# Loading the modulation weights from GpSimd's queue, and token-major projections with 512 instead of 256 columns per product

## The chip, the cores and the metric

The kernel runs on one core of a Trainium2 chip. A core has TensorE (matrix products, results in PSUM), VectorE, ScalarE and GpSimd, and SyncE (SP), which here only issues DMA transfers. SP, ScalarE and GpSimd each have a queue in program order; an instruction waits there for its semaphores and holds up what stands behind it. The metric is the device time of one execution in microseconds (us).

## The reference

The model has two layers on 256 latent and 256 context tokens of 1024 features. Every layer is a SwiGLU half-step, a token mixer and another SwiGLU half-step; shift, scale and gate of each come from modulation vectors. The mixer is neighbourhood attention beside a Hyena convolution in layer 0, and retention in layer 1.

```python
def modulate(x, gain, shift, scale):
    return rms_norm(x, gain) * (1 + scale) + shift

def swiglu(h, w_in, w_out):
    a, b = jnp.split(h @ w_in, 2, axis=-1)
    return (jax.nn.silu(a) * b) @ w_out
...
    for i in range(DEPTH):
        mod_l = (jax.nn.silu(c) @ w_mod[i] + b_mod[i]).reshape(b, N_MOD, 1, D_MODEL)
        mod_c = (jax.nn.silu(c_ctx) @ w_mod[i] + b_mod[i]).reshape(N_MOD, 1, D_MODEL)
        x_lat = x_lat + 0.5 * mod_l[:, 2] * swiglu(modulate(x_lat, norm_gain[i, 0], mod_l[:, 0], mod_l[:, 1]),
                                                 ffn_a_in[i], ffn_a_out[i])
...
def retention_mixer(h_lat, h_ctx, w_in, w_out, logit_f, logit_b, rope_cos, rope_sin, ctx_out):
    def project(hh):
        q, k, v, g = jnp.split(hh @ w_in, [RET_QK, 2 * RET_QK, 2 * RET_QK + RET_V], axis=-1)
...
    def output(y, g, dtype):
...
        return (jax.nn.silu(g) * y) @ w_out
```

Only the latent stream of the last layer is returned.

## The kernel before

**Layout.** Activations lie feature-major: a tile has 128 features on the partitions and 512 columns, 256 latent and 256 context tokens. The normalised input of a layer's part is `H`, 8 such blocks, each as a pair of fp32r tiles, `hhi` (rounded) and `hlo` (the rest). Weights are split likewise into `whi` and `wlo`. Every product of two split operands is three products of TensorE: hi by hi, hi by lo, lo by hi (`mm3`, lines 208 to 210; the third of them is the first that reads `wlo`).

**Weights.** All weight tiles come in one order (`worder`). `w_dma` loads a tile of 512 or 704 KB into one of 4 `raw` buffers by SP's queue (line 138). `w_split` has ScalarE write `whi` and VectorE `wlo` (lines 152 and 153; 4 buffers each). `w_get` hands a tile to TensorE and has the splits issued up to three tiles ahead.

**FFN.** `ffn` goes through two halves of 11 pairs of weight tiles. `in_tile` makes one 128 x 512 product of a tile with `H`, in PSUM as `pi` (24 products of TensorE). `evac` has ScalarE and VectorE make `sg`, then split it into `ghi` and `glo`, so that 11 gate tiles collect. `out_gemm` multiplies them with 8 out-tiles, in the order of the gate tiles: the last gate tile is read by the products 31 to 33 of each out-tile.

**Modulation.** Layer 0's first shift and scale are made by TensorE at the start (`mods`). The other 128 tiles of modulation weights, 128 x 1024 each, are reduced by VectorE: `mod_step` multiplies a tile `wm` with the conditioning vector `scb`, one instruction per stream (line 237, output `junk`). The calls lie between the pairs of the FFN (two steps each) and behind the first four out-tiles of `out_gemm`. `m_dma` loads a tile into one of two buffers; `mod_step` calls it right after the reductions, for the tile after this one, so a tile's load is written in the program one step ahead of its use. In the first FFN, steps begin once the Hyena filter's tables have been split (`parted`, line 637), which GpSimd's four subtractions `flo` do.

**Token-major projections.** Three projections are wanted with tokens on the partitions: the values of the attention (`mixer0`, around line 1149), and values and gates of each retention head (`tok_proj`, line 1316, called by `tiles`). There `H` is the stationary operand, 128 features by 128 tokens, and the weights move. A weight tile of 128 x 1024 holds four blocks of features by 256 columns, as `tok_tiles` in `_layout` lays it out on the host; two tiles cover the 1024 features of one half of the 512 columns. For a head, four weight tiles make the values of four token tiles (`pv`), four more the gates of two (`pg`), with the scores of the next head and the output of this one between.

**Order.** Each engine runs its instructions in the order in which this program writes them; nothing reorders them later.

Of the kernel before, what the change touches and what calls it, by code (L numbers as in the profile page):

```python
# [16 lines left out]
P = 128  # L17
D = 1024
KB = D // P
# [35 lines left out]
def body(ctx, tc, I, out):  # L55
    nc = tc.nc
    V, S, T, SY, G = nc.vector, nc.scalar, nc.tensor, nc.sync, nc.gpsimd
# [16 lines left out]
    def page(shape=None, dt=F32, name="page"):  # L74
        tag = free.pop(0)
        low[0] = min(low[0], len(free))
        t = pagep.tile(shape or [P, TOK], dt, tag=tag, name=name)
        held[id(t)] = (tag, t)
        return t
# [5 lines left out]
    def ps(shape=None, name="ps"):  # L85
        return psp.tile(shape or [P, 512], F32, tag="ps", name=name)
# [55 lines left out]
    def w_split():  # L142
        i = wpos["split"]
        if i >= len(worder):
            return
        while wpos["dma"] <= i:
            w_dma()
        n = worder[i][1]
        t = raws.pop(i)
        hi = whl.tile([P, WSLOT], F32R, tag="hi", name="whi")  # L150
        lo = whl.tile([P, WSLOT], F32R, tag="lo", name="wlo")
        act(hi[:, :n], t[:, :n], AF.Copy)
        V.tensor_tensor(out=lo[:, :n], in0=t[:, :n], in1=f(hi[:, :n]), op=ALU.subtract)  # L153
        hls[i] = (hi, lo)
        wpos["split"] += 1
        if not hold[0]:
            w_dma()
# [14 lines left out]
    def w_get(ahead=3):  # L172
        i = wpos["get"]
        while wpos["split"] <= min(i + ahead, len(worder) - 1):
            w_split()
        wpos["get"] += 1
        return hls.pop(i)
# [39 lines left out]
    def m_dma():  # L217
        n = mpos["dma"]
        if n >= len(mlist):
            return  # L220
        t = modp.tile([P, D], F32, tag="wm", name="wm")
        SY.dma_start(out=t, in_=I["wmt"][n])
        mtile[n] = t
        mpos["dma"] += 1

    def mod_step(n=1):
        for _ in range(n):
            i = mpos["get"]
            if i >= len(mlist):
                return  # L230
            while mpos["dma"] <= i:
                m_dma()
            l, idx, b = mlist[i]
            t = mtile.pop(i)
            bcol = cst[:, C_BMOD + l * 72 + idx * 8 + b:C_BMOD + l * 72 + idx * 8 + b + 1]
            for s in range(1 if (l == 1 and idx >= 5) else 2):
                V.tensor_tensor_reduce(out=junk, in0=t, in1=scb[:, s, :], scale=1.0, scalar=bcol,  # L237
                                       op0=ALU.mult, op1=ALU.add,
                                       accum_out=MOD[l][:, idx, b, s:s + 1])
            mpos["get"] += 1  # L240
            m_dma()
# [669 lines left out]
    def mixer0(norm_in, norm_out):  # L911
# [34 lines left out]
        def z_conv(j, p, first):  # L946
            c = conv(p, (4 if first else 8) + j, "x1c" if first else "vc")
            b = next(c)
            yield
            next(c, None)  # L950
            if first:
                z[j] = b
                return
            V.tensor_tensor(out=z[j], in0=z[j], in1=b, op=ALU.mult)
            drop(b)
# [170 lines left out]
        def qk_step(again=False):  # L1126
            if todo:
                w, pp = todo.pop(0)
                sq = sqs.pop(0)
                if todo:  # L1130
                    sqs.append(qk_sq(todo[0][1]))
                qk_norm(w, pp, sq, ps(name="qss") if again else pso.tile([P, 512], F32, tag="po", name="qss"))
# [7 lines left out]
        pv = [ps(name="pv") for _ in range(4)]  # L1140
        for c in range(2):
            w = [w_get(), w_get(2)]
            for tb in range(4):
                o = pv[tb][:, c * 256:(c + 1) * 256]
                hs_ = slice(tb * P, (tb + 1) * P)
                for k in range(KB):
                    wk = w[k // 4]
                    ws_ = slice(k % 4 * 256, (k % 4 + 1) * 256)
                    T.matmul(o, lhsT=H[k][0][:, hs_], rhs=wk[0][:, ws_], start=k == 0, stop=False)
                    T.matmul(o, lhsT=H[k][0][:, hs_], rhs=wk[1][:, ws_], start=False, stop=False)  # L1150
                    T.matmul(o, lhsT=H[k][1][:, hs_], rhs=wk[0][:, ws_], start=False, stop=k == KB - 1)
                if c == 0 and tb in (0, 2):
                    qk_step()
# [33 lines left out]
        for i in range(12):  # L1187
            p = in_tile()
            attend(i)
            if i < 8:  # L1190
                ex, nor = left.pop(0)
                c = z_conv(i // 2, p, i % 2 == 0)
# [26 lines left out]
        for i in range(2):  # L1219
            t = page(dt=F32R, name="dfthi"), page(dt=F32R, name="dftlo")  # L1220
# [13 lines left out]
        for s in range(2):  # L1234
            for cb in range(4):
                inv(cb, s, py[cb])
                if s:
                    t = x0c[cb].rearrange("p s t -> p (s t)")
# [8 lines left out]
        out_gemm([cat[i] for i in range(KB)], KB, 1, 0, 1, False, norm_out)  # L1247

    mixer0(nm[0, 1], nm[0, 2])
    ffn(0, 2, nm[0, 2], nm[1, 0])  # L1250
    ffn(1, 0, nm[1, 0], nm[1, 1])


    def mixer1(norm_in, norm_out):
# [32 lines left out]
        for h in range(4):  # L1287
            pa, pb = in_tile(0, L), in_tile(0, L)
            q = page(name="qT")
# [23 lines left out]
            return dl, dc  # L1313


        def tok_proj(ntb, po, w, kh):
            for tb in range(ntb):
                for k4 in range(4):
                    k = kh * 4 + k4
                    hs_ = slice(tb * P, (tb + 1) * P)  # L1320
                    ws_ = slice(k4 * 256, (k4 + 1) * 256)
                    T.matmul(po[tb], lhsT=H[k][0][:, hs_], rhs=w[0][:, ws_], start=k == 0, stop=False)  # L1322
                    T.matmul(po[tb], lhsT=H[k][0][:, hs_], rhs=w[1][:, ws_], start=False, stop=False)  # L1323
                    T.matmul(po[tb], lhsT=H[k][1][:, hs_], rhs=w[0][:, ws_], start=False, stop=k == KB - 1)  # L1324
# [28 lines left out]
            return pt  # L1353

        def tiles(ntb, po, n):
            c, kh = divmod(n, 2)
            tok_proj(ntb, [q[:, c * 256:(c + 1) * 256] for q in po], w_get(), kh)

        def pv_norm(h, qb, pt, vh):
            p = ps(name="po")  # L1360
# [43 lines left out]
        for h in range(4):  # L1404
            if h < 3:
                qk_parts(h + 1)
            pv = [ps(name="pv") for _ in range(4)]
            for n in range(4):
                tiles(4, pv, n)
                if n == 0 and prev:  # L1410
                    o_trans(h - 1, prev)
            vh = []
            for tb in range(4):
                vh.append((page(dt=F32R, name="vhi"), page(dt=F32R, name="vlo")))
                split_to(pv[tb], *vh[tb])
            pg = [ps(name="pg") for _ in range(2)]
            tiles(2, pg, 0)
            if h < 3:
                npt = scores(h + 1)
            tiles(2, pg, 1)  # L1420
            os = [pv_norm(h, qb, pt, vh) for qb in range(2)]
            tiles(2, pg, 2)
            tiles(2, pg, 3)
            for a in vh + pt:
                drop(*a)
            for qb in range(2):
                gate_mul(os[qb], pg[qb])
            S.preload_act_table_set(LOG_SET)
            prev = os
            pt = npt  # L1430
# [16 lines left out]
    for b in range(KB):  # L1447
        c = slice(b % 2 * L, (b % 2 + 1) * L)
# [4 lines left out]
def _layout(inp):  # L1453
# [27 lines left out]
    t = np.linspace(0.0, 1.0, L, dtype=f4)  # L1481
    w = (f4(2.0 * math.pi) * np.arange(L, dtype=f4) / f4(L)).astype(f4)
# [28 lines left out]

    def tok_tiles(w):
        C = w.shape[1]
        return w.reshape(2, 4, P, C // 256, 256).transpose(3, 0, 2, 1, 4).reshape(C // 256 * 2, P, D)

    we = g["even_in"][0]
    fe = feat_tiles(we, 0)
# [1 line left out]
    hyo = [16, 20, 17, 21, 18, 22, 19, 23, 12, 13, 14, 15]  # L1519
    eo = g["even_out"][0]  # L1520
    z["ev"] = np.concatenate([fe[order], tok_tiles(we[:, 1024:1536]), fe[hyo], feat_tiles(eo, 0)])
    wr = g["ret_in"][0]
    perm = np.concatenate([h * 256 + np.concatenate([np.arange(64), 128 + np.arange(64), 64 + np.arange(64),
                                                     192 + np.arange(64)]) for h in range(4)])
    wq, wk = wr[:, :1024][:, perm], wr[:, 1024:2048][:, perm]
    vt, gt = tok_tiles(wr[:, 2048:4096]), tok_tiles(wr[:, 4096:6144])
    wo = g["ret_out"][0]
    o2 = np.stack([feat_tiles(wo[:D], 0), feat_tiles(wo[D:], 0)], axis=1).reshape(16, P, D)
# [14 lines left out]
    r, c = np.divmod(np.arange(L), 64)  # L1543
# [34 lines left out]
```

## Time and profile before

| | before |
|---|---|
| median of 3 runs | 1894.0 us (1890.67 to 1895.0) |
| profiled execution | 1885.11 us |
| its span, first to last instruction | 1883.3 us |
| TensorE busy | 1862.5 us, 99% of the span |
| VectorE busy | 1206.5 us, 64% |
| ScalarE busy | 701.3 us, 37% |
| GpSimd busy | 65.6 us, 3% |
| transfers of `wm` tiles for VectorE | 128 of 512 KB, all from SP's queue |
| transfers issued by GpSimd | 8 of 256 KB |

Busy is the time in which at least one instruction of an engine runs, from the start to the modelled end of each. Products on TensorE overlap, so that the distance of their starts, not their duration, tells how many fit in a stretch. A wait is counted when an engine has nothing running; "idle" in brackets behind an instruction is such a wait, with what ended it.

### The profile page before, as it was taken

How to read it: one execution, taken by the hardware profiler on the slowest of the kernel's cores; microseconds unless marked ns; L12 is line 12 of the kernel's file. 1: busy time of each engine (PE TensorE's matmuls, PEld its weight loads, DVE VectorE, ACT ScalarE, POOL GpSimd, SP SyncE). 2: the span in 40 equal slices, each digit the busy share in tenths (PEclk: the TensorE clock that was granted, in tenths of full speed). 3: DMA queues.
4: the chain of work that ended last, by engine and by line, in shares of the span. 5: the costliest groups of instructions: out<-in, count | busy, mean ns of one | idle time of the engine just before them, and what ended most of it. 6: DMA issues, size and time to landing. Idle time of an engine off the chain costs nothing.

```text
span 1883.3 us, 26318 instructions
## 1 busy us (share of the span) xinstructions
PE 1862.5 (99%) x10646; PEld 1607.7 (85%) x10646; DVE 1206.5 (64%) x1858; ACT 701.3 (37%) x1085; POOL 65.6 (3%) x73
## 2 busy tenths in 40 slices
PE   8999999999999999999999999999999999999999
PEld 5788888798877898788878988888889999999999
DVE  5577677777687767776766655433356755567554
ACT  4332122245474342212223422122234454455342
POOL 1010000002003000000000000000000111000000
PEclk9999999999999999999999999999999999999999
DMA  9345455532323325554564356323323423355663
GB/s 362 129 168 190 163 173 178 201 108 79 101 68 101 134 80 185 191 183 157 179 208 138 112 194 220 101 89 109 105 83 103 133 90 101 103 182 186 192 185 130
DMA packets 77899, 277.52 MB, mean 147 GB/s; under 512 B 8657, under 2 KB 9681, under 8 KB 77650
## 3 DMA queue, kind: packets, MB, share of 16 engines
q1 hardware_dynamic: 76626, 273.76, 43.7%
q0 software_dynamic: 1152, 2.10, 0.4%
q8 instruction: 83, 1.36, 0.3%
q14 instruction: 38, 0.31, 0.0%
HBM read 274.77 MB, written 1.05 MB: 146 GB/s over the span
## 4 chain that ended last, share of the span: by engine, by line
PE 84%; DVE 6%; DMA 6%; issue 2%; ACT 1%; SPq 0%; POOL 0%; DVEq 0%; POOLq 0%; ACTq 0%
PE pi L208 12%; PE pi L209 12%; PE pi L210 12%; PE po L209 9%; PE po L210 9%; PE po L208 9%; DMA wm<-in_wmt_dram 6%; DVE wlo L153 3%; PE fg L208 2%; PE fg L210 2%; PE fg L209 2%; PE pv L1322 2%; PE pv L1323 2%; PE pv L1324 2%; DVE junk L237 1%
## 5 line engine op out<-in xcount | busy, mean ns | idle before, releaser
L208 PE MATMUL pi<-hhi,whi 128*128 128x512 f32 (+1 forms) x1488 | 544.2, 366 | 0.0
L209 PE MATMUL pi<-hlo,whi 128*128 128x512 f32 (+1 forms) x1488 | 543.9, 366 | 0.0
L210 PE MATMUL pi<-hhi,wlo 128*128 128x512 f32 (+1 forms) x1488 | 543.1, 365 | 0.0
L153 DVE TENSOR_TENSOR wlo<-raw,whi 128x1024 fp32r<-128x1024 f32 (+1 forms) x325 | 421.5, 1313 | 164.3 <-ACT whi L89 164.1
L89 ACT ACTIVATE whi<-raw 128x1024 fp32r<-128x1024 f32 (+1 forms) x329 | 364.3, 1116 | 399.2 <-PE po L209 160.5
L237 DVE CUSTOM_DVE_ANT_0 junk<-wm,scb,cst 128x1024 bf16<-128x1024 f32 x224 | 291.1, 1299 | 84.0 <-DMA wm<-in_wmt_dram 80.1
L208 PEld LDWEIGHTS pi<-hhi,whi 128*128 128x128 f32 x1488 | 279.3, 188 | 51.7 <-issue 1.5
L210 PEld LDWEIGHTS pi<-hhi,wlo 128*128 128x128 f32 x1488 | 279.3, 188 | 48.8
L209 PEld LDWEIGHTS pi<-hlo,whi 128*128 128x128 f32 x1488 | 279.4, 188 | 48.1
L208 PE MATMUL po<-ghi,whi 128*128 128x512 f32 (+1 forms) x770 | 269.3, 350 | 1.1 <-ACT ghi L89 1.1
L209 PE MATMUL po<-glo,whi 128*128 128x512 f32 (+1 forms) x770 | 268.4, 349 | 0.7 <-DVE glo L181 0.7
L210 PE MATMUL po<-ghi,wlo 128*128 128x512 f32 (+1 forms) x770 | 268.4, 349 | 0.0
L89 ACT ACTIVATE ghi<-sg 128x512 fp32r<-128x512 f32 (+1 forms) x88 | 50.9, 579 | 378.8 <-DVE sg L580 375.7
L208 PEld LDWEIGHTS po<-ghi,whi 128*128 128x128 f32 x770 | 144.8, 188 | 22.2 <-ACT ghi L89 2.0
L209 PEld LDWEIGHTS po<-glo,whi 128*128 128x128 f32 x770 | 144.9, 188 | 21.9 <-DVE glo L181 1.6
L210 PEld LDWEIGHTS po<-ghi,wlo 128*128 128x128 f32 x770 | 144.9, 188 | 20.2
L391 DVE SCALAR_TENSOR_TENSOR x<-po,gate,x 128x256 f32<-128x256 f32 x136 | 61.3, 480 | 120.5 <-PE po L210 120.2
L580 DVE TENSOR_TENSOR sg<-sg,pi 128x512 f32<-128x512 f32 (+1 forms) x79 | 49.1, 621 | 104.3 <-PE pi L210 102.7
L181 DVE TENSOR_TENSOR glo<-sg,ghi 128x512 fp32r<-128x512 f32 (+1 forms) x88 | 55.1, 626 | 56.9 <-ACT ghi L89 56.9
L89 ACT ACTIVATE sq<-x 128x256 f32<-128x256 f32 (+1 forms) x71 | 30.2, 439 | 115.7 <-DVE x L391 115.6
L1322 PE MATMUL pv<-whi,hhi 128*128 128x256 f32 x256 | 72.2, 282 | 0.0
L1323 PE MATMUL pv<-wlo,hhi 128*128 128x256 f32 x256 | 71.7, 280 | 0.0
(332 smaller groups left out, 2392.1 us busy)
## 6 DMA issues: line engine op xcount, KB each, us to landing
raw<-in_ffi_dram SPq DMA_DIRECT2D x176, 512.0 KB, 3.7
wm<-in_wmt_dram SPq DMA_DIRECT2D x128, 512.0 KB, 4.4
raw<-in_ffo_dram SPq DMA_DIRECT2D x64, 704.0 KB, 4.4
raw<-in_rt_dram SPq DMA_DIRECT2D x64, 512.0 KB, 3.7
raw<-in_ev_dram SPq DMA_DIRECT2D x32, 512.0 KB, 3.5
wm<-in_wm_dram SPq DMA_DIRECT2D x32, 256.0 KB, 5.6
x<-in_xt_dram SPq DMA_DIRECT2D x8, 256.0 KB, 5.0
bias<-in_rpb_dram SPq DMA_DIRECT2D x8, 256.0 KB, 4.0
```

Source lines behind the costliest of these rows:

```text
L89: S.activation(out=out, in_=in_, func=func, **k)
L153: V.tensor_tensor(out=lo[:, :n], in0=t[:, :n], in1=f(hi[:, :n]), op=ALU.subtract)
L181: V.tensor_tensor(out=lo, in0=src, in1=f(hi), op=ALU.subtract)
L208: T.matmul(o, lhsT=w[0][:, c0:c1], rhs=x[0][:, x0:x1], start=start, stop=False)
L209: T.matmul(o, lhsT=w[0][:, c0:c1], rhs=x[1][:, x0:x1], start=False, stop=False)
L210: T.matmul(o, lhsT=w[1][:, c0:c1], rhs=x[0][:, x0:x1], start=False, stop=stop)
L237: V.tensor_tensor_reduce(out=junk, in0=t, in1=scb[:, s, :], scale=1.0, scalar=bcol, op0=ALU.mult, op1=ALU.add, accum_out=MOD[l][:, idx, b, ...
L391: V.scalar_tensor_tensor(out=xs(s, m), in0=p[:, c0:c0 + L], scalar=gate[:, m, s:s + 1], in1=xs(s, m), op0=ALU.mult, op1=ALU.add)
L580: V.tensor_tensor(out=sg, in0=sg, in1=pb[:, :w], op=ALU.mult)
L1322: T.matmul(po[tb], lhsT=H[k][0][:, hs_], rhs=w[0][:, ws_], start=k == 0, stop=False)
L1323: T.matmul(po[tb], lhsT=H[k][0][:, hs_], rhs=w[1][:, ws_], start=False, stop=False)
L1324: T.matmul(po[tb], lhsT=H[k][1][:, hs_], rhs=w[0][:, ws_], start=False, stop=k == KB - 1)
```

## The change

The loads of modulation tiles are issued by GpSimd's queue (`G`) instead of SP's (`SY`). And in the three token-major projections a product takes 512 columns of weights instead of 256: a weight tile now holds two blocks of features by 512 columns, and four tiles cover the 1024 features of all 512 columns. The number of weight tiles and their size stay; the accumulators are the same.

```diff
@@ def m_dma
         t = modp.tile([P, D], F32, tag="wm", name="wm")
-        SY.dma_start(out=t, in_=I["wmt"][n])
+        G.dma_start(out=t, in_=I["wmt"][n])
@@ mixer0
             for tb in range(4):
-                o = pv[tb][:, c * 256:(c + 1) * 256]
+                o = pv[tb]
                 hs_ = slice(tb * P, (tb + 1) * P)
-                for k in range(KB):
-                    wk = w[k // 4]
-                    ws_ = slice(k % 4 * 256, (k % 4 + 1) * 256)
+                for k in range(4 * c, 4 * c + 4):
+                    wk = w[k // 2 % 2]
+                    ws_ = slice(k % 2 * 512, (k % 2 + 1) * 512)
@@ mixer1
-        def tok_proj(ntb, po, w, kh):
+        def tok_proj(ntb, po, w, kq):
             for tb in range(ntb):
-                for k4 in range(4):
-                    k = kh * 4 + k4
+                for k2 in range(2):
+                    k = kq * 2 + k2
                     hs_ = slice(tb * P, (tb + 1) * P)
-                    ws_ = slice(k4 * 256, (k4 + 1) * 256)
+                    ws_ = slice(k2 * 512, (k2 + 1) * 512)
...
         def tiles(ntb, po, n):
-            c, kh = divmod(n, 2)
-            tok_proj(ntb, [q[:, c * 256:(c + 1) * 256] for q in po], w_get(), kh)
+            tok_proj(ntb, po, w_get(), n)
@@ def _layout, tok_tiles
-        return w.reshape(2, 4, P, C // 256, 256).transpose(3, 0, 2, 1, 4).reshape(C // 256 * 2, P, D)
+        return w.reshape(4, 2, P, C // 512, 512).transpose(3, 0, 2, 1, 4).reshape(C // 512 * 4, P, D)
```

TensorE's order in the first weight tile of head 0's values, before: the last products of the first token tile (`pv_11775`) and the first of the second (`pv_11776`); a number behind a name tells buffers apart.

```order
L1322 MATMUL pv_11775<-whi_11596,hhi_10926 128x256
L1323 MATMUL pv_11775<-wlo_11597,hhi_10926 128x256
L1324 MATMUL pv_11775<-whi_11596,hlo_10927 128x256
L1322 MATMUL pv_11775<-whi_11596,hhi_10928 128x256
L1323 MATMUL pv_11775<-wlo_11597,hhi_10928 128x256
L1324 MATMUL pv_11775<-whi_11596,hlo_10929 128x256
L1322 MATMUL pv_11776<-whi_11596,hhi_10922 128x256
L1323 MATMUL pv_11776<-wlo_11597,hhi_10922 128x256
L1324 MATMUL pv_11776<-whi_11596,hlo_10923 128x256
```

The same place now, all of the first token tile (`pv_11679`) and the first products of the second:

```order
L1322 MATMUL pv_11679<-whi_11500,hhi_10826 128x512
L1323 MATMUL pv_11679<-wlo_11501,hhi_10826 128x512
L1324 MATMUL pv_11679<-whi_11500,hlo_10827 128x512
L1322 MATMUL pv_11679<-whi_11500,hhi_10828 128x512
L1323 MATMUL pv_11679<-wlo_11501,hhi_10828 128x512
L1324 MATMUL pv_11679<-whi_11500,hlo_10829 128x512
L1322 MATMUL pv_11680<-whi_11500,hhi_10826 128x512
L1323 MATMUL pv_11680<-wlo_11501,hhi_10826 128x512
L1324 MATMUL pv_11680<-whi_11500,hlo_10827 128x512
```

A weight tile meets two blocks of `H` per token tile where it met four, with products twice as wide.

GpSimd's order in the first FFN and after it, as a difference: the filter's last two subtractions, the loads, and the first work of `mixer0` (`qsqlo`, then tables `dfthi`).

```order
 L637 TENSOR_TENSOR flo<-hsum,fhi 128x512
 L637 TENSOR_TENSOR flo<-hdif,fhi 128x512
+L222 DMA wm<-in_wmt_dram 128x1024 x49
 L933 TENSOR_TENSOR qsqlo<-qsq,qsqhi 128x512 x8
 L630 DMA dfthi<-in_dft_dram 128x512
```

The first 49 loads now stand behind the filter's subtractions and ahead of `mixer0`'s; the other 79 stand behind all of `mixer0`'s subtractions and ahead of those of `mixer1`.

SP's order in the first FFN, before (`raw` are the weight tiles):

```order
L138 DMA raw<-in_ffi_dram 128x1024 x9
L222 DMA wm<-in_wmt_dram 128x1024 x3
L138 DMA raw<-in_ffi_dram 128x1024 x2
L222 DMA wm<-in_wmt_dram 128x1024 x2
L138 DMA raw<-in_ffi_dram 128x1024 x2
L222 DMA wm<-in_wmt_dram 128x1024 x2
```

Now:

```order
L138 DMA raw<-in_ffi_dram 128x1024 x4
L883 DMA scb<-in_cc_dram 128x2048
L138 DMA raw<-in_ffi_dram 128x1024 x14
L138 DMA raw<-in_ffo_dram 128x1408 x8
L138 DMA raw<-in_ffi_dram 128x1024 x22
```

The `raw` loads keep their order, and no `wm` load stands between them.

## Rows read from the trace of the kernel before

**Rows 1.** The page: busy time by engine, and the chain of work by line.
```profile
PE 1862.5 (99%) x10646; PEld 1607.7 (85%) x10646; DVE 1206.5 (64%) x1858; ACT 701.3 (37%) x1085; POOL 65.6 (3%) x73
...
PE pi L208 12%; PE pi L209 12%; PE pi L210 12%; PE po L209 9%; PE po L210 9%; PE po L208 9%; DMA wm<-in_wmt_dram 6%; DVE wlo L153 3%; PE fg L208 2%; PE fg L210 2%; PE fg L209 2%; PE pv L1322 2%; PE pv L1323 2%; PE pv L1324 2%; DVE junk L237 1%
```

**Rows 2.** TensorE's waits: who waited for whom, us in total, times, longest.
```profile
PE ptc L1074 <- DVE prc L1054: 2.5, 1, 2.5
...
PE po L208 <- ACT ghi L89: 1.1, 1, 1.1
...
PE po L209 <- DVE glo L181: 0.7, 3, 0.2
```

**Rows 3.** Groups by line and shape: count, busy us, mean ns, idle before.
```profile
L208 PE MATMUL pi<-hhi,whi 128*128 128x512 f32 x1120 | 441.4, 394 | 0.0
...
L237 DVE CUSTOM_DVE_ANT_0 junk<-wm,scb,cst 128x1024 bf16<-128x1024 f32 x224 | 291.1, 1299 | 84.0 <-DMA wm<-in_wmt_dram 80.1
...
L1322 PE MATMUL pv<-whi,hhi 128*128 128x256 f32 x256 | 72.2, 282 | 0.0
...
L1322 PE MATMUL pg<-whi,hhi 128*128 128x256 f32 x128 | 35.9, 281 | 0.0
```

**Rows 4.** Timeline of TensorE, FFN then retention: start us, duration us, instruction.
```profile
712.58 0.39 PE L210 MATMUL pi<-hhi,wlo 128*128 128x512 f32 x1
...
729.97 0.40 PE L210 MATMUL pi<-hhi,wlo 128*128 128x512 f32 x1
...
1476.93 0.28 PE L1322 MATMUL pv<-whi,hhi 128*128 128x256 f32 x1
...
1499.44 0.28 PE L1324 MATMUL pv<-whi,hlo 128*128 128x256 f32 x1
```

**Rows 5.** Windows, retention heads: PE, PEld, DVE, ACT, POOL busy; PEclk, DMA, GB/s.
```profile
1476.90:1655.00 178.10, 178.10 (x1422) 173.78 (x1421) 101.62 (x163) 85.04 (x129) 14.38 (x9) 1.00 0.30 96
```

**Rows 6.** Timeline of VectorE and SP in the second layer-0 FFN.
```profile
716.39 1.28 DVE L237 CUSTOM_DVE_ANT_0 junk<-wm,scb,cst 128x1024 bf16<-128x1024 f32 x1
...
723.03 0.43 SPq L222 DMA_DIRECT2D wm<-in_wmt_dram  x1
...
726.21 1.28 DVE L237 CUSTOM_DVE_ANT_0 junk<-wm,scb,cst 128x1024 bf16<-128x1024 f32 x1
...
729.69 1.29 DVE L237 CUSTOM_DVE_ANT_0 junk<-wm,scb,cst 128x1024 bf16<-128x1024 f32 x1 [0.87 <-DMA wm<-in_wmt_dram]
```

**Rows 7.** Timeline of VectorE and TensorE at the end of the first FFN's pairs.
```profile
349.95 1.28 DVE L237 CUSTOM_DVE_ANT_0 junk<-wm,scb,cst 128x1024 bf16<-128x1024 f32 x1 [2.73 <-DMA wm<-in_wmt_dram]
...
355.57 0.68 DVE L580 TENSOR_TENSOR sg<-sg,pi 128x512 f32<-128x512 f32 x1
...
356.96 0.51 PE L208 MATMUL po<-ghi,whi 128*128 128x512 f32 x1 [1.07 <-ACT ghi L89]
357.69 0.50 PE L209 MATMUL po<-glo,whi 128*128 128x512 f32 x1 [0.22 <-DVE glo L181]
```

**Rows 8.** Timeline of GpSimd, VectorE and TensorE where the modulation steps begin.
```profile
96.22 1.30 POOL L637 TENSOR_TENSOR flo<-hsum,fhi 128x512 fp32r<-128x512 f32 x1 [52.74 <-ACT fhi L89]
...
96.25 2.35 DVE L237 CUSTOM_DVE_ANT_0 junk<-wm,scb,cst 128x1024 bf16<-128x1024 f32 x1
...
105.25 2.35 DVE L153 TENSOR_TENSOR wlo<-raw,whi 128x1024 fp32r<-128x1024 f32 x2
...
112.45 0.39 PE L210 MATMUL pi<-hhi,wlo 128*128 128x512 f32 x1
```

**Rows 9.** Landing by line: L630 (GpSimd) at 570; at 15; L222 at 91; all L222.
```profile
DMA to landing us min/median/max: 3.9/4.3/4.5
...
DMA to landing us min/median/max: 6.2/7.9/9.8
...
DMA to landing us min/median/max: 3.7/4.0/4.4
...
DMA to landing us min/median/max: 3.3/4.4/8.1
```

## Prediction

> **What bounds the kernel now.** I read the shares of the engines and the chain of work first, then the waits of TensorE, then the timeline, since the shares mislead here. TensorE is busy for 1862.5 of 1883.3 us, and VectorE, the next, for 1206.5 [rows 1]. The chain of work consists mostly of TensorE's lines, but 6% of the span in it is DMA of the modulation tile `wm` and 3% VectorE's weight split `wlo` [rows 1]. That looks like 110 us to be had from the loads. The list of TensorE's waits says otherwise: what it waited for on that account is 1.1 us for `ghi` and 0.7 us for `glo`, and its longest wait, 2.5 us for `prc`, is in the attention stage, where no `wm` is loaded [rows 2]. So VectorE sits idle 80.1 us for `wm` [rows 3] while TensorE has work queued. **The bound is the rate at which TensorE takes products.**
>
> That rate can't be read from durations. A product with 512 columns is shown as 394 ns and one with 256 as 281 or 282 ns [rows 3], and they overlap. The distance from start to start can be read: between the two rows of the FFN lie 75 steps in 17.39 us, 231.9 ns each; between the two of the retention stage 191 steps in 22.51 us, 117.9 ns each [rows 4]. There TensorE is busy for 178.10 of 178.10 us at a granted clock of 1.00, the 2.4 GHz level [rows 5].
>
> **Part one, 512 columns per product.** The products with 256 columns number 256 + 128 for each of the three lines of `tok_proj` [rows 3], so 1152, and 2 x 4 x 8 x 3 = 192 in the value projection of `mixer0`. 1344 become 672 of 512 columns, with as many weight loads. Two of the old cost 2 x 117.9 = 235.8 ns, one of the new 231.9 if it runs as the FFN's, which has the same form (a 128 x 128 stationary operand, 512 moving columns in SBUF): 3.9 ns a pair. In `tok_proj` that is 576 x 3.9 = 2.2 us, all on the path, as TensorE does not wait there. Each weight tile still costs the same time (48 x 117.9 = 5.66 us, or 24 x 231.9 = 5.57 us), each accumulator is completed by the fourth tile as before, and the same splits and evictions follow, so the cover of ScalarE's and VectorE's work shrinks by 0.1 us in 5.6. In `mixer0`, 96 x 3.9 = 0.4 us; the 2.5 us wait for `prc` behind it [rows 2] can swallow some, and I take half. Together 2.4 us; the ends are 2.2 and 2.6.
>
> The Trainium skill (TensorE: Matmul & The Clock Gate, section "Back-to-back issue gap") gives a spacing of columns / 2.4 GHz + 2.5 ns for an isolated stream, which makes a pair worth 2.5 ns and this part an estimated 1.7 us; 117.9 and 231.9 ns [rows 4] lie above both of its values (109.2 and 215.8 ns) and I go by the rows. The same section states about 131 ns a product at 512 columns as a sustained rate; that would make the part an estimated 70 us, and 231.9 ns [rows 4] contradicts it.
>
> **Part two, `wm` by GpSimd's queue.** The 128 loads of 512 KB are the same; another queue issues them. On SP a `wm` load stands behind two `raw` loads, each of which waits for VectorE to finish with the buffer. So in the FFN loop the load at 723.03 went out late, and VectorE stood idle 0.87 us for it at 729.69 [rows 6]. On GpSimd's queue it waits only for the last reader of its own buffer: the reduction that began at 716.39 ended at 717.67, and the next step with that buffer begins at 726.21 [rows 6], a window of 8.5 us. GpSimd's own 256 KB loads in a quiet stretch landed after 3.9 to 4.5 us, SP's 512 KB `wm` loads after 3.3 to 8.1, median 4.4 [rows 9]. I take 4.5 for the new ones: they fit, and the 80.1 us of idle VectorE should fall to a few.
>
> What TensorE gets of that: where the `wm` waits have pushed VectorE behind, its last `sg` comes late (355.57, after the wait that ended at 349.95), and TensorE waits for `ghi` and `glo` at 356.96 and 357.69 [rows 7]. All such waits sum to 1.1 + 0.7 = 1.8 us in four places [rows 2]; idle time is counted from the shown end of a product, 394 - 232 = 162 ns after the next could have started, so four more times 0.16 us: 2.4 us. Without lag nothing takes their place: one pair of FFN tiles takes TensorE 48 x 231.9 ns = 11.1 us, and VectorE's work per pair is two weight splits (2.35), two evictions (0.7 each) and four reductions (1.28 each), 8.9 us. Ends: 0 and 2.7. Behind a waiting load on GpSimd's queue stand only further `wm` loads, until the `qsqlo` of `mixer0`, long after; SP loses 128 waits and nobody waits for that.
>
> **The start of part two** is the one place where the move costs. In the program GpSimd does four `flo` subtractions just ahead of the first `wm` load, while SP had nothing ahead of it. Before, VectorE's first reduction began at 96.25, just when the first `flo` did [rows 8]. Now the load is issued after the subtractions: 96.22 + 4 x 1.30 = 101.4. The reduction waits for it, lands at 101.4 + 4.5 = 105.9, four reductions and one weight split follow (4 x 1.28 + 1.2 = 6.3; the long ones, 2.35 us [rows 8], ran beside GpSimd's), so that `wlo` is ready at 112.2 instead of 106.4. TensorE needs it at 112.45, in the third product of its tile [rows 8]. So the cover is nearly used up: I take 0. The bound on the other side is the slowest of GpSimd's first loads, 9.8 us after issue with the DMA engines full [rows 9]: then 117.5 us, a stall of 5.1.
>
> **The sum:** -2.4 - 2.4 + 0 = -4.8 us on a profiled execution of 1885.1 us (span 1883.3 and 1.8 around it). The runs before have a median of 1894.0 us, 0.5% above the profiled one; I subtract the same 4.8 us: **1889.2 us**, 0.25% less, where about 0.2%, 3.8 us, is what a measurement of this kernel can tell from no change.
>
> **Rivals.**
> *The first load is late* (0.16): it lands after 9.8 instead of 4.5 us. For it: one of GpSimd's first loads did [rows 9]. Against it: in the stretch around 96 us SP has few loads, and its own `wm` loads landed there in 3.7 to 4.4 us [rows 9]. -4.8 + 5.1 = +0.3: 1894.3.
> *The four waits stay* (0.09), because something besides `wm` makes `sg` late: -2.4, 1891.6.
> *GpSimd and VectorE hold each other up* (0.08). The trace shows it in one direction: a reduction takes 2.35 us beside a GpSimd subtraction and 1.28 otherwise [rows 6, 8]. If issuing a load likewise had to wait out a reduction, each would land 1.3 us later. In the loop 4.5 + 1.3 still fits in 8.5 us; at the start `wlo` would be ready at 113.5, a stall of 1.05: -3.75, 1890.3. The Trainium skill (SBUF — State Buffer, section "SBUF: two separate sides") warns of this: a load issued from GpSimd can't have its descriptors written while VectorE runs an instruction that takes both ports for one operand, and it advises ACT's or SP's queue, against this change. It names copies as such instructions, and no copy runs in these loops.
> *Slower: loads land too late in every pair* (0.06). Its point: two reductions and the landing, 2.6 + L, must fit into 11.1 us. At L = 9.8 [rows 9] each pair loses 1.3 us; over the 11 + 9 + 11 pairs of three FFN loops 40 us, of which each loop can hide 7.0 (30 products pass before the out-product reads the last gate tile), so 19; with 5.1 at the start and 2.4 gained, +22: 1916. It decides from L = 9.2 us. Against it: the quiet GpSimd loads and SP's median are less than half of that [rows 9].
> *A product costs its shown duration* (0.01): 672 x (2 x 281 - 394) = 113 us less, 1781. The starts speak against it [rows 4].
> That the change does not do what it says is excluded by the order of instructions: 672 products fewer, and all 128 loads on GpSimd.
>
> **How the numbers follow.** My forecast has 0.60, with 1887 to 1891 of its own. For the range I take the sum's ends, -2.6 - 2.7 = -5.3 (1888.7) and +0.3 (1894.3), and the spread of the runs before about their median (-3.3, +1.0): 1885.0 to 1895.5. Left out are the slower case and the last one. Faster by more than 0.2% means below 1890.2: 0.50 of the forecast, 0.02 of the case just above and 0.01 of the last, 0.53. Slower: 0.06. The same: 0.41.
>
> **What would show it.** The starts of products in `tok_proj` 232 ns apart; VectorE's idle time for `wm` below 15 us from 80.1, most of it at 96 us; no TensorE wait for `ghi` or `glo`; GpSimd's first `wm` issue near 101.4 us and TensorE at the tile of 112 us waiting under 1 us. I am wrong if products of 512 columns stand further than 235.8 ns apart, if TensorE's wait there is several us, or if VectorE waits for `wm` in every pair.

## The result, and the profile after

| | before | after |
|---|---|---|
| median | 1892.97 us (4 runs, 1890.67 to 1895.0) | 1879.63 us (4 runs, 1878.30 to 1880.72) |
| profiled execution, its span | 1885.11, 1883.3 us | 1878.30, 1876.5 us |
| after over before | | 0.9930, 95% interval 0.9914 to 0.9946 |

The change is worth 13.3 us, 0.7%. The forecast was 4.8 us and 1889.2, and its range began at 1885.0: the sign was right, the size was not. The two profiled executions differ by 6.8 us. Against the profiled execution of before the same sum gives 1880.3 us, 0.7 us off the median after. So the question is what the runs before had lost beyond their profiled execution.

The page of after, first the busy times, then the chain of work, then two groups that answer to [rows 1, 3] and the landing times (line, tile, queue, count, KB, median us):

```profile
PE 1857.1 (99%) x9974; PEld 1574.5 (84%) x9974; DVE 1205.4 (64%) x1858; ACT 701.5 (37%) x1085; POOL 131.0 (7%) x201
...
PE 96%; DVE 2%; ACT 1%; issue 0%; DMA 0%; POOL 0%; DVEq 0%; ACTq 0%; POOLq 0%
...
L237 DVE CUSTOM_DVE_ANT_0 junk<-wm,scb,cst 128x1024 bf16<-128x1024 f32 x224 | 287.3, 1283 | 14.1 <-DMA wm<-in_wmt_dram 9.0
...
L222 POOL DMA_DIRECT2D wm<-in_wmt_dram x128 | 67.7, 529 | 785.5 <-DVE mod L237 766.2
...
raw<-in_ffi_dram SPq DMA_DIRECT2D x176, 512.0 KB, 4.2
wm<-in_wmt_dram POOLq DMA_DIRECT2D x128, 512.0 KB, 3.8
raw<-in_ffo_dram SPq DMA_DIRECT2D x64, 704.0 KB, 5.4
```

TensorE has 672 products fewer. VectorE's idle time for `wm` fell from 80.1 to 9.0 us, and the 6% of DMA are gone from the chain. A load costs GpSimd 529 ns to issue and lands after 3.8 us.

TensorE's waits after (waited for: us, times, longest), from the longest that [rows 2] shows down to the only one left for `po`:

```profile
PE ptc L1074 <- DVE prc L1054: 2.5, 1, 2.5
...
PE po L210 <- DVE wlo L153: 0.2, 1, 0.2
```

The waits for `ghi` and `glo` are gone.

### The profile page after: what moved, and what is told of

It reads as the page before. It is cut to its first block, busy times and chain, and to the rows that moved or that the text cites. A ratio compares the mean times of both kernels' runs of the same rounds, so it can differ in the third digit from the quotient of the medians.

```text
span 1876.5 us, 25048 instructions
## 1 busy us (share of the span) xinstructions
PE 1857.1 (99%) x9974; PEld 1574.5 (84%) x9974; DVE 1205.4 (64%) x1858; ACT 701.5 (37%) x1085; POOL 131.0 (7%) x201
## 3 DMA queue, kind: packets, MB, share of 16 engines
q0 software_dynamic: 19584, 69.21, 11.7%
## 4 chain that ended last, share of the span: by engine, by line
PE 96%; DVE 2%; ACT 1%; issue 0%; DMA 0%; POOL 0%; DVEq 0%; ACTq 0%; POOLq 0%
PE pi L208 16%; PE pi L209 16%; PE pi L210 16%; PE po L210 9%; PE po L208 9%; PE po L209 9%; PE fg L208 2%; PE fg L210 2%; PE fg L209 2%; PE pv L1323 2%; PE pv L1324 2%; PE pv L1322 2%; PE pg L1324 1%; PE pg L1323 1%; PE pg L1322 1%
## 5 line engine op out<-in xcount | busy, mean ns | idle before, releaser
L237 DVE CUSTOM_DVE_ANT_0 junk<-wm,scb,cst 128x1024 bf16<-128x1024 f32 x224 | 287.3, 1283 | 14.1 <-DMA wm<-in_wmt_dram 9.0
L222 POOL DMA_DIRECT2D wm<-in_wmt_dram x128 | 67.7, 529 | 785.5 <-DVE mod L237 766.2
L208 PE MATMUL fg<-hhi,whi 128*128 128x256 f32 (+1 forms) x200 | 60.0, 300 | 0.0
```

The costliest lines, as they stand in the source:

```text
L208: T.matmul(o, lhsT=w[0][:, c0:c1], rhs=x[0][:, x0:x1], start=start, stop=False)
L222: G.dma_start(out=t, in_=I["wmt"][n])
```

## Which half of the change does it

All ratios are to runs of the kernel before on the same chip (medians 1892.5 to 1893.6 us there).

**The kernel before, once more** (e1_before): no edit.

> The kernel before, unchanged, profiled once more. Its earlier profiled execution had a span of 1883.3 us, its timed runs a median of 1893.0. Theory A (VectorE's lag behind the modulation loads costs more in most executions than in the profiled one): where the span is near 1891 us, TensorE waits at the heads of out_gemm in the FFNs that have modulation steps, for ghi and glo, 6 to 10 us in sum instead of 1.8. Rival B (the gain comes from the products): TensorE's waits are as in the first profile and the starts of products with 256 columns lie over 125 ns apart.

1891.09 us, ratio 0.9998 (0.9983 to 1.0012). Its profiled execution, 1890.86 us, is a typical one; the one that the prediction read was near the lower end. The 27 other runs of before lay between 1884.7 and 1898.9. TensorE's waits at the heads of `out_gemm` are listed as

```profile
PE po L208 <- ACT ghi L89: 2.5, 3, 1.6
...
PE po L209 <- DVE glo L181: 0.7, 3, 0.2
```

That is 3.2 us, more than the 1.8 us of the first profile, but half of the 6 to 10 us expected.

**The queue alone** (e2_queue).

```diff
-        SY.dma_start(out=t, in_=I["wmt"][n])
+        G.dma_start(out=t, in_=I["wmt"][n])
```

> The kernel before with the modulation loads on GpSimd's queue and nothing else (256 columns stay). Theory A: it has most of the gain, 8 to 11 us below the kernel before, ratio near 0.995. Rival B: it gains at most 2.4 us, ratio 0.999 or more.

1882.20 us, 0.9952 (0.9932 to 0.9972): 10 us less, four times the 2.4 of the prediction, with all times within 3 us of each other.

**The load written one step earlier, on SP's queue** (e5_lead2).

```diff
-            while mpos["dma"] <= i:
+            while mpos["dma"] <= i + 1 and mpos["dma"] < len(mlist):
```

> The kernel before, with the modulation loads on SP's queue as before but written one step earlier, so that a load is issued as soon as the reduction that used its buffer is done and not behind the next two weight tiles. If it is the late issue that costs (theory A), this gives the same as the change of queue, 8 to 11 us less, and VectorE's idle time for wm falls from 80 us to under 15. If it is something about the queue itself (a rival C: fewer loads share SP's ring, weight tiles land earlier), it gives clearly less than the change of queue.

1882.85 us, 0.9951 (0.9934 to 0.9968), the same as GpSimd's queue. No VectorE wait for `wm` is listed. So it is the late issue that cost, and GpSimd's queue has no worth or price of its own that these runs can tell.

**The columns alone** (e3_cols): the change without its first hunk.

> The changed kernel with the modulation loads back on SP's queue, so that only the 512 columns differ from the kernel before. Theory A: 2.4 us less (672 pairs of products at 3.9 ns, less what mixer0 takes back), ratio 0.9985 to 0.9990. Rival B: 8 to 11 us less, ratio near 0.995.

1883.15 us, 0.9962 (0.9945 to 0.9978), with times from 1878.5 to 1890.4: more than the 2.4 us expected, and taken up again below.

**Both halves, in two ways**: the changed kernel itself (f3_after), and 512 columns with the earlier load on SP (f4_cols_lead2), on one chip.

> The changed kernel as it is, for a comparison on one chip. About 1879.6 as measured before, ratio 0.993. Its times lie within 3 us of each other, as it has no waits at the heads of out_gemm.

> 512 columns in all three projections, modulation tiles on SP but written one step earlier. If only the late issue mattered and not the queue: the same as the changed kernel within 2 us, about 1880, no VectorE wait for wm in the loops and no TensorE wait for ghi or glo at the heads of out_gemm. If GpSimd's queue had a worth of its own: 3 us or more slower than the changed kernel.

1879.06 us (0.9926) and 1879.23 us (0.9927), each within 2 us. On top of the queue alone, measured on another chip, the columns are worth 3.1 us (in the profiled executions 1878.9 us of span against 1876.5 of after and 1877.7 of f3_after).

## Where the 10 us were: the lag of VectorE, and the clock behind it

The profiled execution of e3_cols shows the loss well. SP, VectorE and TensorE at the end of the first FFN's second half; a number in brackets is the idle time ahead, with what ended it:

```profile
342.40 1.86 SPq L138 DMA_DIRECT2D raw<-in_ffo_dram  x2
344.32 4.47 SPq L222 DMA_DIRECT2D wm<-in_wmt_dram  x2
...
349.19 0.39 PE L210 MATMUL pi<-hhi,wlo 128*128 128x512 f32 x1
...
353.25 1.28 DVE L237 CUSTOM_DVE_ANT_0 junk<-wm,scb,cst 128x1024 bf16<-128x1024 f32 x1 [4.82 <-DMA wm<-in_wmt_dram]
...
358.86 0.68 DVE L580 TENSOR_TENSOR sg<-sg,pi 128x512 f32<-128x512 f32 x1
360.24 0.69 DVE L181 TENSOR_TENSOR glo<-sg,ghi 128x512 fp32r<-128x512 f32 x1 [0.69 <-ACT ghi L89]
...
360.26 0.80 PE L208 MATMUL po<-ghi,whi 128*128 128x512 f32 x1 [3.77 <-ACT ghi L89]
```

The `wm` loads go out behind two `raw` loads of 704 KB. VectorE waits 4.82 us, its last `glo` is ready at 360.93, 11.7 us behind the start of the pair's last product (349.19; this distance is the lag in what follows), and TensorE stands still for 3.77 us. The same place after:

```profile
344.78 0.53 POOL L222 DMA_DIRECT2D wm<-in_wmt_dram  x1 [2.13 <-DVE mod L237]
...
347.78 0.39 PE L210 MATMUL pi<-hhi,wlo 128*128 128x512 f32 x1
...
349.67 0.69 DVE L181 TENSOR_TENSOR glo<-sg,ghi 128x512 fp32r<-128x512 f32 x1 [0.70 <-ACT ghi L89]
```

Here `glo` ends 350.36 - 347.78 = 2.6 us behind. Worked out in the same way from the timelines, the lag at the last pair of the four halves that carry modulation steps, and what TensorE's first two late starts there lie beyond their usual distance:

| profiled execution | lag in the four halves, us | TensorE beyond its pace, us | length of two stretches, us |
|---|---|---|---|
| before (1885.1) | 5.2, 9.0, 7.9, 7.8 | 2.7 | 616.9 |
| e1_before (1890.9) | 6.8, 8.5, 9.6, 8.3 | 4.5 | 620.2 |
| h2_order (1893.2) | 6.0, 10.4, 7.5, 10.2 | 6.1 | 623.2 |
| e3_cols (1888.2) | 4.9, 11.7, 8.6, 5.2 | 5.7 | 622.3 |
| after, e2_queue, e5_lead2, f3_after, f4_cols_lead2 | 2.6 in each | 0 | 613.8 |

(h2_order is the kernel before with its inputs declared in another order; it comes up below.) The last column adds the stretch from the first `po` product of the first FFN to the first `fg` product behind that FFN, and the stretch between the first `fg` products of the second FFN and of the next. Their ends in h2_order, then in e2_queue:

```profile
167.56 0.39 PE L208 MATMUL po<-ghi,whi 128*128 128x512 f32 x1
...
416.93 0.28 PE L208 MATMUL fg<-hhi,whi 128*128 128x256 f32 x1
...
671.54 0.28 PE L208 MATMUL fg<-hhi,whi 128*128 128x256 f32 x1
...
1045.41 0.28 PE L208 MATMUL fg<-hhi,whi 128*128 128x256 f32 x1
```

```profile
166.18 0.39 PE L208 MATMUL po<-ghi,whi 128*128 128x512 f32 x1
...
410.75 0.28 PE L208 MATMUL fg<-hhi,whi 128*128 128x256 f32 x1
...
663.77 0.28 PE L208 MATMUL fg<-hhi,whi 128*128 128x256 f32 x1
...
1032.98 0.28 PE L208 MATMUL fg<-hhi,whi 128*128 128x256 f32 x1
```

Without lag the two stretches take 613.8 us in all five executions; with it they take 3.1, 6.4, 9.4 and 8.5 us more.

Up to a lag of some 7 us the 30 products ahead of the last gate tile hide everything (6.8 us cost nothing in e1_before, 7.8 us cost 0.4 in before); the kernel before runs at 5 to 12 us, on the edge, and where it falls differs from one execution to the next.

And a stall costs more than itself. Windows of e3_cols (start:end, length, busy us of PE, PEld, DVE, ACT, POOL, granted clock, DMA share, GB/s), before, right behind and after the 3.77 us wait; then one of e1_before, behind a wait of 1.61 us at 801.34, and one of before, behind the 1.07 us of [rows 7]:

```profile
350.00:356.00 6.00, 6.00 (x28) 4.90 (x27) 2.71 (x5) 0.00 (x0) 0.00 (x0) 1.00 0.25 93
359.40:366.20 6.80, 5.94 (x13) 4.46 (x14) 3.34 (x6) 1.90 (x2) 0.00 (x0) 0.54 0.88 325
366.30:373.00 6.70, 6.70 (x29) 5.41 (x28) 6.63 (x10) 2.08 (x3) 0.00 (x0) 0.97 0.25 88
```

```profile
802.30:805.70 3.40, 3.40 (x9) 2.63 (x9) 2.21 (x4) 1.63 (x2) 0.00 (x0) 0.51 0.84 301
```

```profile
357.50:361.00 3.50, 3.31 (x14) 2.74 (x15) 2.63 (x5) 0.68 (x1) 0.00 (x0) 1.00 0.92 336
```

The granted clock falls to the 1.2 GHz level (0.50): 13 products in 6.80 us (5.94 of them busy), against 29 in 6.70. It does not fall behind every wait: in before it stays at 1.00. The Trainium skill (TensorE: Matmul & The Clock Gate, section "HAM oscillation — how this bites in real kernels") tells of the same: waits between groups of products let the clock fall, at a price of half the slow time. The rows of e3_cols and e1_before agree, with 0.54 and 0.51 behind the waits.

**A lag made on purpose.** Into the changed kernel, ahead of the last pair's evacuation in each of the four halves, go four or eight more reductions on VectorE (h3_extra4, h4_extra8).

```diff
                 pb = in_tile(0, w)
+                if l == 0 and j == NH - 1:
+                    for _ in range(4):          # 8 in h4_extra8
+                        V.tensor_tensor_reduce(out=junk, in0=scb[:, 0, :], in1=scb[:, 1, :], ..., accum_out=spare)
                 evac(pa, pb)
```

> The changed kernel with four more reductions on VectorE (scb with scb, into junk, 1.28 us each) ahead of the evacuation of the last pair in each FFN half of layer 0, so in four places. The last split of glo comes 4 x 1.28 = 5.1 us later, 7.7 us behind the pair's last product instead of 2.6. Theory (the first 30 products of out_gemm hide a lag of about 7.3 us, and only what is beyond stalls TensorE): 0.2 to 0.5 us a place, 1 to 2 us in all, 1880 to 1881. If the lag cost from its first microsecond: 20 us more, 1900.

> The same with eight more reductions in each of the four places: 12.9 us of lag, 5.6 beyond what is hidden. If a stall costs only itself: 4 x 5.6 = 22 us, 1901. If the granted clock falls to the 1.2 GHz level behind such a stall, as it did behind the 4.8 us stall at 360 us in the kernel with 512 columns alone: 1.7 to 3.4 us more in each place, 1908 to 1915, and the trace shows four stretches of 0.50 behind the four stalls.

The lags, expected at 7.7 and 12.9 us, came out at 6.9, 6.9, 6.9, 4.9 us with four and 12.2, 12.2, 12.2, 10.2 us with eight. Waits of TensorE for `po` with four, then with eight, and windows of the latter:

```profile
PE po L210 <- DVE wlo L153: 0.2, 1, 0.2
```

```profile
PE po L208 <- ACT ghi L89: 14.6, 4, 4.2
...
PE po L209 <- DVE glo L181: 0.5, 2, 0.2
...
178.50:181.80 3.30, 3.30 (x8) 2.27 (x9) 3.23 (x6) 2.44 (x2) 0.00 (x0) 0.50 0.02 5
182.00:185.30 3.30, 3.30 (x16) 2.63 (x15) 3.26 (x6) 0.00 (x0) 0.90 (x2) 1.00 0.49 159
369.60:372.80 3.20, 3.20 (x8) 2.43 (x8) 3.13 (x5) 0.25 (x1) 0.53 (x1) 0.50 0.00 0
...
816.80:823.40 6.60, 5.83 (x13) 4.33 (x14) 5.80 (x11) 3.28 (x3) 0.53 (x1) 0.50 0.13 25
1007.90:1011.10 3.20, 3.20 (x9) 2.46 (x8) 3.16 (x5) 0.16 (x1) 1.05 (x2) 0.50 0.26 41
```

With four there is no stall; with eight there are four, and a stretch of 0.50 behind each. Both kernels hold one more small buffer, which by itself costs 8 us (last section), so they stand against j2_shift, 1887.1: 1887.85 with four, +0.7 for 16 reductions; 1913.6 with eight. From four to eight that is 25.8 us (27.7 us of span). The waits shown are 14.6 + 0.5, with eight times 0.16 us 16.4. The four stretches at 0.50 last at least 16.3 us, so that half, some 8 us, goes to the clock. The other 3.3 us of the 27.7 lie elsewhere: half of a stretch of 3.2 us at 0.50 at 523 us, behind the wait for `prc` in the attention stage, and half of one of 3.4 us at 632 us in the filter, neither of which h3_extra4 has:

```profile
523.20:526.40 3.20, 3.20 (x16) 2.87 (x16) 2.70 (x6) 1.76 (x4) 0.00 (x0) 0.50 0.25 49
...
632.00:635.40 3.40, 3.40 (x18) 3.40 (x18) 1.88 (x3) 0.63 (x1) 0.00 (x0) 0.50 0.27 110
```

So the mechanism and its price are shown: 24 us for four lags of 10 to 12 us. They also explain most of the 10 us of the typical kernel before: its two stretches took 6.4 us more than without lag in e1_before and 9.4 in h2_order. The remainder is not the lag's. Of the 10.2 us of span between e1_before and e2_queue, 2.2 arose before the first out-product, which lies at 165 to 168 us in all these kernels, and 1.5 between the two stretches. There a slow clock behind the wait for `prc` comes in some executions and not in others, with lag or without; the profiled execution after has it:

```profile
506.50:510.00 3.50, 3.50 (x18) 3.17 (x19) 3.04 (x7) 1.75 (x4) 0.00 (x0) 0.54 0.24 50
```

## The columns: 2.5 us in their stage, and a rest that stays open

**mixer0 alone, the retention stage alone** (f1_cols_mix0, f2_cols_ret; the latter again as j4_cols_ret on another chip): the second hunk of the change, or the third and fourth, each with the new layout for its weights only.

> 512 columns per product in the value projection of mixer0 alone (96 products fewer), everything else as before, modulation tiles on SP. Theory A (a product saves 3.9 ns per pair and nothing else): 96 x 3.9 = 0.4 us, so within 1 us of the kernel before, about 1892. Theory B (the projection's new order changes the waits around it, at 450 to 510 us, and whether the granted clock falls behind the wait for prc near 510): about 3 to 6 us faster, and no fall of the clock near 510 us in the trace. Under both, the waits for ghi at the heads of out_gemm stay and the times scatter by 10 us or more.

> 512 columns per product in the retention stage alone (576 products fewer), mixer0 as before, modulation tiles on SP. Theory A: 576 x 3.9 = 2.2 us faster, about 1890. Theory B (mixer0's order is what gave the 512-column kernel its 8 us): the same 2.2 us here, so about 1890 too, and the rest in the kernel that changes mixer0 alone. Theory C (something in the retention stage other than the spacing, a wait that its tiles had): 6 us or more, and a wait there that is gone.

> 512 columns in the retention stage alone, once more. If the earlier 1882.8 was the chip or chance: 1890, as the spacing says. If it belongs to the program: 1883 again, 9 to 10 below the kernel before of the same call.

1890.61 us (0.9985, 0.9971 to 0.9999), 1882.76 us (0.9954, 0.9939 to 0.9968; expected 1890) and 1885.60 us (0.9967, 0.9953 to 0.9981; expected 1890 or 1883, and between the two). mixer0 alone, predicted at 0.2 to 0.4 us, is within its interval of that. In the traces the gain of the retention stage is close to what was predicted. The last out-products of the input FFN of layer 1 begin here, before and after:

```profile
1344.42 0.39 PE L208 MATMUL po<-ghi,whi 128*128 128x512 f32 x1
```

```profile
1340.25 0.39 PE L208 MATMUL po<-ghi,whi 128*128 128x512 f32 x1
```

From there to the end of the span it is 538.9 us before and 536.3 after; e1_before, e2_queue and e5_lead2 also have 538.9, f2_cols_ret, e3_cols and j4_cols_ret 536.2 to 536.3. That is 2.6 us for the predicted 2.2. The rest of the 7 to 11 us came ahead of this point, where the program is the same, down to the place of each buffer: taking these lengths off, the median of the part ahead is 1345 to 1348 us in these three and 1352 to 1353 in before. The single profiled executions do not show the difference: the two FFN stretches took 616.4 us in f2_cols_ret, 620.5 in j4_cols_ret and 622.3 in e3_cols, so these kernels lag as well, and before has 616.9 to 623.2. Two tries at the cause:

**Fewer products with 256 columns** (h1_fewer, j3_len).

```diff
                     T.matmul(po[tb], lhsT=H[k][0][:, hs_], rhs=w[0][:, ws_], ...)
-                    T.matmul(po[tb], lhsT=H[k][0][:, hs_], rhs=w[1][:, ws_], ...)   # j3_len: kept for odd k only
-                    T.matmul(po[tb], lhsT=H[k][1][:, hs_], rhs=w[0][:, ws_], ...)
```

In h1_fewer only the third product is left out.

> The kernel before (256 columns, modulation tiles on SP) without the third product (line 1324) in the token-major projections of the retention stage, so that 384 products of 256 columns are left out there. 384 x 117.9 = 45.3 us. Theory A (each stage costs what its products cost): 1892.5 - 45.3 = 1847. Theory D (a program with fewer TensorE instructions in the retention stage also loses less in the FFNs that run before it, as the runs with 512 columns in that stage showed about 6 us more than the spacing gives): 1841, with the end of the first mixer's FFN earlier than before in the trace.

> The kernel before (256 columns, SP's queue) with 576 products of the retention projections left out: all of the third kind (line 1324) and every other one of the second (line 1323), so that it has as many TensorE instructions as the kernel with 512 columns there. The retention stage will wait for other engines; its own length is read from the trace and taken off. Theory D (fewer instructions in the program make the FFNs before it lag less): what is left, the part up to the end of the mixer of layer 1's input FFN, is 6 us shorter than in the kernel before, as with 512 columns. If it is not: that part is as long as before, about 1350 us with a scatter of 10.

**Another place in memory** (h2_order): the inputs are declared in the reverse order.

> The kernel before with its input tensors declared in the reverse order, nothing else. If the place of the weights in memory decides how late the modulation tiles land, the time moves by several us, either way, and the scatter too; if it does not, 1892 within 3 us, with the same waits for ghi.

h1_fewer: 1857.96 us, of which 503.7 lie behind the point, so 1352.5 ahead, as before. (It saved 36 and not 45 us, in part because the stage then waits for VectorE, 4.6 us for `on` at `pot` alone.) j3_len: 1843.89 us, 495.0 behind, 1347.1 ahead: shorter, like the kernels with 512 columns, in only 4 runs. h2_order: 1891.68 us, 0.9990 (0.9976 to 1.0003), no effect. So the column width seems not to be needed for it, as far as four runs can tell, and the number of instructions alone doesn't explain it either, since h1_fewer has 384 fewer and f1_cols_mix0, at about 1350, 96. What makes the lag smaller in some programs stays open. It is bounded: without the lag (e2_queue to the changed kernel) the columns bring some 3 us.

## Why the prediction was wrong, step by step

- **Part one, 512 columns: right.** 231.9 ns a product were taken over from the FFN; the starts give 231.3 in `tok_proj` after, 95 steps in 21.97 us (answering to [rows 4]), and the stage is 2.6 us shorter for a predicted 2.2.

```profile
1472.76 0.40 PE L1322 MATMUL pv<-whi,hhi 128*128 128x512 f32 x1
...
1494.73 0.39 PE L1324 MATMUL pv<-whi,hlo 128*128 128x512 f32 x1
```

- **The four waits, 2.4 us: mis-sized.** They vanished as said, and VectorE's idle time fell below 15 us as said. But 1.8 + 4 x 0.16 us (four waits, at three heads of `out_gemm`) was the price in one execution with little lag, whose two FFN stretches lost 3.1 us. Others stall longer, 4.5 us in e1_before and 6.1 in h2_order, and the term left out what a stall does to the clock: 6.4 and 9.4 us in the stretches. The queue alone measured 10.3 us.
- **"I subtract the same 4.8 us": the step that failed.** The profiled run lay 8.9 us below the median, and the prediction took that for a constant offset. It was, for the most part, the scatter of the very stalls that the change removes: without lag the times lie within 1.4 us (f3_after) and 3 us (e2_queue), with it within 11 to 16 on each chip. The part had to be subtracted from the profiled time, where it gives 1880.3. That this falls so near the median after is in part luck: the two profiled executions differ by 6.8 us and not 4.8 (0.8 at the start, 3.1 in the FFN stretches, 0.3 between them, 2.6 behind), and the profiled execution after lies 1.3 us below its own median.
- **The range.** Its ends add up to 1885.4 and 1895.3, set down as 1885.0 and 1895.5. The spread came from three runs, down to 3.3 us below their median; the 27 runs beside e1_before reach 7.8 below theirs. A spread caused by the stalls would also have had to shrink with them.
- **The start of part two: right, at 0.** GpSimd and VectorE there after (answering to [rows 8]):

```profile
99.17 1.31 POOL L637 TENSOR_TENSOR flo<-hdif,fhi 128x512 fp32r<-128x512 f32 x1
100.41 1.16 POOL L222 DMA_DIRECT2D wm<-in_wmt_dram  x2
...
104.50 1.29 DVE L237 CUSTOM_DVE_ANT_0 junk<-wm,scb,cst 128x1024 bf16<-128x1024 f32 x1 [8.98 <-DMA wm<-in_wmt_dram]
...
109.69 2.36 DVE L153 TENSOR_TENSOR wlo<-raw,whi 128x1024 fp32r<-128x1024 f32 x2
```

  The load went out at 100.41 (predicted 101.4, on a clock that began 0.8 us later) and the first `wlo` was ready at 110.9; VectorE's 8.98 us are all of its idle time for `wm`, and TensorE lists no wait there.
- **The rivals.** The first load was not late. The four waits went. GpSimd and VectorE do not hold each other up: GpSimd issues a load in 529 ns, its loads land after 3.8 us against 3.5 on SP's queue in e5_lead2, not 1.3 us later, and SP's queue with the earlier load gives the same time (f4_cols_lead2). The Trainium skill's warning (SBUF — State Buffer, section "SBUF: two separate sides") therefore did not bite here; it names copies, and the loops have none. Loads late in every pair: the median landing was 3.8 us, far from the 9.2 at which that case began.

## What to carry to other kernels

Before a profiled execution's waits are taken as a price, see how the times scatter and where this execution lies among them. Where a helper's lag sits at the edge of what hides it, the scatter is itself the loss, and a change that removes the lag brings every run down to about the lowest times seen, less the stalls that these still had. Price a TensorE stall together with the slow clock that can follow it.

## What the runs showed of the hardware

**The place of buffers in SBUF moves the pace of products.** One more 4-byte buffer ahead of the activation pages, never read, moves all pages of the changed kernel by 32 bytes in the program's layout (j2_shift); in j1_aligned all pages lie at multiples of 64 bytes.

```diff
+    spare = one.tile([P, 1], F32, name="spare")      # j2_shift
+    V.memset(spare, 0.0)
...
-            b = page([P, 2, L + 2], F32R, "uhi"), page([P, 2, L + 2], F32R, "ulo")      # j1_aligned
+            b = page([P, 2, L + 8], F32R, "uhi"), page([P, 2, L + 8], F32R, "ulo")
...
-    sml = ctx.enter_context(tc.tile_pool(name="sml", bufs=6))
+    sml = ctx.enter_context(tc.tile_pool(name="sml", bufs=5))
```

> The changed kernel with one more 4-byte buffer ahead of the pages, set to zero once and never read, which moves all pages by 32 bytes; no extra reductions. Theory P: the products stand 1.5 ns further apart, as in the kernel with four extra reductions, 7 to 9 us over the changed kernel, 1886 to 1888. If the extra reductions themselves slowed the products down: 1879.

> The changed kernel with every page buffer at a multiple of 64 bytes in SBUF: the eight wider pages hold 264 instead of 258 columns per row, and the small pool has 5 instead of 6 buffers to make room. In the traces products whose moving operand lies at 32 beyond a multiple of 64 bytes stand 1.1 ns (pi, 656 products) and 2.0 ns (po, 427) further from the next than the others. Theory P (the place decides): 0.7 + 0.9 us less, 1877 to 1878 against 1879.1. If the place does nothing: 1879.

j2_shift: 1887.11 us, 0.9974 (0.9962 to 0.9985), 8 us over the changed kernel, which was measured on another chip (1879.06; 6.0 us more span in the profiled executions). First and last product of the 528 in a half, of f3_after and then of j2_shift:

```profile
228.84 0.40 PE L208 MATMUL pi<-hhi,whi 128*128 128x512 f32 x1
...
350.36 0.39 PE L210 MATMUL pi<-hhi,wlo 128*128 128x512 f32 x1
```

```profile
228.46 0.39 PE L208 MATMUL pi<-hhi,whi 128*128 128x512 f32 x1
...
350.99 0.40 PE L210 MATMUL pi<-hhi,wlo 128*128 128x512 f32 x1
```

121.52 and 122.53 us for 527 steps: 230.6 and 232.5 ns, without a wait. It is not the chip: j4_cols_ret, with the pages unmoved, has 230.6 ns there on the chip of j2_shift, and h3_extra4 has 232.5 on another. j1_aligned took 1881.36 us, 0.9945 (0.9926 to 0.9963), on another chip than f3_after: no faster. Its products of 512 columns in the FFNs stood 230.6 to 231.4 ns apart, as near as after or nearer, but those of 256 columns in the last FFN 118.2 instead of 116.9. So the place decides up to 0.8% of a product of 512 columns, but "a multiple of 64 bytes" is not the whole rule, and which one it is stays open. A spacing carried to another kernel is only as good as that: the pace was 230.6 ns in one FFN and 231.9 in another of the same execution.

No version tried here that does all the products is faster than the changed kernel by more than the runs can tell.
